# Keys and queries interleaved in DRAM and loaded with one transfer per operand, and the first stage of a hybrid attention layer in another order

## The chip, the cores and the metric

The kernel runs on one core of a Trainium2 chip. The metric is the device time of one launch, in microseconds (us), as the median of several runs; profiles are of one execution. The core has five engines that work side by side, each through its own instructions in order: TensorE (PE, matmuls and transposes; its weight loads are listed as PEld), VectorE (DVE), ScalarE (ACT), GpSimd (POOL), and SyncE (SP), which here does nothing but issue DMA transfers. A DMA issue on SP waits for the eighth issue before it, because eight hardware counters are used in turn.

## What is computed

The reference is one inference step of an encoder layer, on a prompt of 2048 tokens and a sample of 64 tokens that attends to 512 cached ones. It is cut here to what matters:

```python
h = rmsnorm(x, g_pre)
fq, fk, fv, ff, fg, dq, dk, dv, dg = split(h @ w_in)          # widths 512, ff: 8
logf = log_sigmoid(ff + b_f); cum = cumsum(logf)
# group A, 8 heads of 64: forgetting attention, causal
s = fq . fk / 8 + cum[query] - cum[key];      fox = softmax(s) fv
# group B, 4 heads, two halves of 64 for queries and keys, values of 128, causal by chunks of 64
p = softmax(q1 . k1 / 8 + t5_bias) - lam * softmax(q2 . k2 / 8 + t5_bias)
diff = rmsnorm(p dv, subln) * (1 - lam_init)
y = x + rmsnorm(concat(fox * silu(fg), diff * silu(dg)) @ w_out, g_post)
```

The outputs are y for the prompt and the sample, and the new rows of fk, fv, logf, dk and dv. Everything is float32. The width of the model is 1024.

## The kernel before, in words

**Precision.** TensorE works here on values rounded to a shorter form, so each operand is split into a rounded part h and the rest l, and a product is made of three matmuls (lines 868 to 870: wh and x's h, wl and x's h, wh and x's l). In the scores a key operand holds h and l of 64 dimensions in its 128 partitions; it is multiplied with a query tile that holds (h|l) and with one that holds (l|h), line 351.

**Stages.** The prompt is four blocks of 512 tokens, each of four tiles of 128; the sample is a fifth tile of block 0. For each block the projection goes through eight groups of 512 columns: fv, fg, fk, fq, dg, dk, dq, dv in the even blocks, reversed in the odd ones. A group has eight slices of 128 input rows; a slice of weights is loaded (`wst` in block 0, `wraw` later, line 773), cast by ACT to `wh` (line 776), and the rest `wl` is made by DVE or POOL (line 777). The tokens' slices `xraw` become `xx` (lines 744 to 748). In block 0 the first group is accumulated for all tiles at once as slices come in; its forget logits follow (lines 1096 and 1097), with sums of squares `ptq` (line 1071), the 1/rms `xrs` (lines 154 to 157) and its transposed copy `ptr` (line 1055), which is written to DRAM (RS) and loaded again over all partitions as `rbc`. In the other blocks the sums of squares come from loads `xn` (lines 1036 and 1037).

**Results on their way.** Evictions (`ef`, line 878) go out, and their h and l parts to scratch in DRAM: keys turned over by TensorE (`ptk`, line 959), split as `khl` and written to KS; values to VS; queries, which leave TensorE already turned, scaled by `rbc` (`qf`), split as `qhl` (lines 1013 to 1017) and written to QD (line 1019); gates to GS; the running sum of log-forget to CUM. `khl`, `qhl` and `vhl` share a pool of two buffers, `ef`, `xn`, `qf` and others one of four. An eviction that takes a buffer waits until the DMA that read it has landed.

**Attention.** A block's attention runs beside the next block's projection; the output projection runs beside the last block's. What to load is asked for per head and pair of query tiles, and queued in rings: K 4 tiles of 1024 keys, V 4, Q 6 tiles of 256 columns, bias 2, gates 2. A K tile takes a load per 512 keys (line 194), a query pair takes one load for (h|l) (line 267) and two of 64 partitions for (l|h) (line 270), a bias tile a load per 512 keys (line 285). All these go through SP's one queue, with the weights and the writes.

**What sets the order.** Every piece of work is put on a line of places measured in TensorE time, and the pieces are issued in that order; a scheduler then orders each engine's instructions. Constants are loaded in `prologue` (place 20) and `prologue2` (place 110): the latter loads `lamt` and `cbias` (lines 1358 and 1370). The forget bias `fb` and the scale `subl` are loaded at the very start from ACT's queue, `fb` with

```python
nc.scalar.dma_start(out=fb, in_=bass.AP(fbias.tensor, fbias.offset, [[0, P], [0, 5], [1, 8]]))
```

which is 128 x 5 = 640 pieces of 32 bytes, and DVE scales `subl` right away (line 119). The output projection's weights `wor` are cast in place of the projection's operands (lines 1199 to 1201) as the last block's attention runs alone.

Of the kernel before, what the change touches and what calls it, by code (L numbers as in the profile page):

```python
# [9 lines left out]
F32 = mybir.dt.float32  # L10
# [7 lines left out]
P = 128  # L18
# [15 lines left out]
# T5 bucket of rel = key - query over the runs of rel in which it is constant  # L34
# (NUM_BUCKETS = 32, MAX_DISTANCE = 128, bidirectional); every rel below -90 is bucket 15.
# [7 lines left out]
LINE = BW + P - 1  # L43


class Ring:
    """Loads that run ahead of their use, as many as there are free slots."""
# [43 lines left out]
def hybrid_step(ctx: ExitStack, tc: tile.TileContext, ins, outs):  # L91
# [23 lines left out]
    fb = cp.tile([P, 40], F32, name="fb")  # L115
    nc.scalar.dma_start(out=fb, in_=bass.AP(fbias.tensor, fbias.offset, [[0, P], [0, 5], [1, 8]]))
    subl = cp.tile([P, 1], F32, name="subl")
    nc.scalar.dma_start(out=subl, in_=subln)
    nc.vector.tensor_scalar(out=subl, in0=subl, scalar1=1.0 - LAM_INIT, scalar2=None, op0=ALU.mult)
# [15 lines left out]
    QD = [dr.tile([2, 8, P, BLK + (DEC if b == 0 else 0)], F32, name=f"QD{b}") for b in range(NBLK)]  # L135
# [4 lines left out]
    CUM = [dr.tile([8, BLK], F32, name=f"CUM{b}") for b in range(NBLK)]  # L140
# [5 lines left out]
    def rsqrt_newton(pool, v, out, rows, n, tag, eng=None):  # L146
        """out = 1/sqrt(v): exp(-ln(v)/2) and one Newton step."""
# [11 lines left out]
    # ------------------------------------------------------------------ attention  # L159
    class Attn:  # L160
        """Attention of one range of query tiles, over every unit (two fox heads or one diff head)."""
# [38 lines left out]
        def want_kc(self, got, u):  # L200
            """The sample's keys of a unit: both heads' operands, the cached ones and the new ones."""
# [13 lines left out]
            def second():  # L215
# [5 lines left out]
                # the order of the parts doesn't matter  # L221
# [38 lines left out]
        def want_q(self, got, u, hd, col, w):  # L260
            def load(s):
                def go():
                    t = self.p["q"].tile([P, 256], F32R, name="qg", tag="q")
                    src = QD[0] if col >= SEQ else QD[col // BLK]
                    c0 = BLK if col >= SEQ else col % BLK
                    if s == 0:
                        nc.sync.dma_start(out=r32(t[:, :w]), in_=src[hd, u, :, c0:c0 + w])
                    else:
                        for a in (0, 64):
                            nc.sync.dma_start(out=r32(t[a:a + 64, :w]), in_=src[hd, u, 64 - a:P - a, c0:c0 + w])  # L270
                    got.append(t)
                return go
            for s in (0, 1):
                self.want(self.Q, load(s))

        def want_cum(self, got, h, nk, sample):
            def load(c0, w):
                def go():
# [3 lines left out]
                    else:  # L282
                        for a in range(c0, c0 + w, BLK):
                            ww = min(BLK, c0 + w - a)
                            nc.sync.dma_start(out=t[:, a - c0:a - c0 + ww],
                                              in_=bcast_row(CUM[a // BLK][h, 0:ww], ww))
# [5 lines left out]
        def want_strip(self, got, h, nk, sample):  # L292
            """The bias of the last columns up to the diagonal; before them it is that of bucket 15."""
# [46 lines left out]
            # chunks of at most a bank, none narrow where that can be avoided  # L340
# [46 lines left out]
        def store_mix(self, mix, u, pair, w):  # L387
            """mix: f32 [128 mix columns, w tokens], in SBUF."""
            nc.sync.dma_start(out=(MN if pair is None else MS[pair])[u], in_=mix[:, :w])

        # ---- sub-jobs: (A thunks, B thunks, thunks of the step after)
        def fox(self, u, hd, pair, ctxu, first, last, sample=False):
            """One head, one pair of query tiles (or the sample's tile)."""
# [7 lines left out]
            for j, t in enumerate(tiles):  # L401
# [14 lines left out]
                if j == len(tiles) - 1:  # L416
                    def endA():
                        self.Q.free(); self.Q.free()
# [1084 lines left out]
```

## Time and profile before

| | us |
|---|---|
| runs | 1832.17, 1841.0, 1841.08 |
| median | 1841.0 |
| span of the profiled execution | 1837.8 |
| PE busy in it | 1736.8 |
| DVE, ACT, POOL busy | 1189.6, 1128.9, 768.2 |
| data moved by DMA | 361.38 MB |

The profiled execution's own time isn't listed apart from its span. How to read the lines further down: a row of the timeline has start and duration in us, engine, line of the kernel, operation, output <- inputs, shapes, and in brackets the idle time of that engine just before it and what ended it (`<-DMA x<-y` is a transfer's landing, `<-ACT ef L878` an instruction on another engine). A row of windows has a stretch, its length, the busy time (and count) of PE, PEld, DVE, ACT and POOL, the clock granted to TensorE as a share of full speed, the mean busy share of the 16 DMA engines, and GB/s. A row for a line, such as L1201, has the least, median and greatest duration in ns. A row of DMA issues has the count, KB each, and the median time to landing.

### The profile page before, as it was taken

The page shows a single profiled execution, that of the slowest core. Times are in us where ns is not written, and L with a number is a line of the kernel's source. Part 1 is how long each engine was busy: PE and PEld are TensorE (multiplying, and loading weights), DVE is VectorE, ACT ScalarE, POOL GpSimd, SP SyncE. Part 2 cuts the span into 40 slices and gives each one's busy share as a digit, 9 for nine tenths or more (in the row PEclk, how much of TensorE's full clock was granted, in tenths as well). Part 3 has the DMA queues.
Part 4 walks back from the last instruction along what each step waited for, and adds up shares of the span by engine and source line. Part 5 has one row for each costly group of instructions (what it writes and reads, how often), then busy time and mean ns, then how long its engine had stood idle before and what let it go on. Part 6 is the DMA issues. An engine that isn't in the chain of part 4 may idle for free. (4 is left out here: it accounts for less than half of the span.)

```text
span 1837.8 us, 31858 instructions
## 1 busy us (share of the span) xinstructions
PE 1736.8 (95%) x9828; PEld 1467.4 (80%) x9828; DVE 1189.6 (65%) x3274; ACT 1128.9 (61%) x2518; POOL 768.2 (42%) x1083
## 2 busy tenths in 40 slices
PE   7888999999999999989999999999989999999998
PEld 5676888777877778878888888888878878887887
DVE  5422555556668576656776678878867876666764
ACT  4533656465767666665666657667776666556663
POOL 2204235345354453343323225555795663322331
PEclk9998999999999999999999999999989999999999
DMA  7787579789868766867777667667665464455433
GB/s 203 240 193 193 162 217 273 205 245 233 218 209 246 213 196 195 233 170 230 219 229 224 177 181 216 195 195 224 199 219 166 145 189 156 153 181 156 145 115 108
DMA packets 308170, 361.38 MB, mean 197 GB/s; under 512 B 41808, under 2 KB 202732, under 8 KB 308000
## 3 DMA queue, kind: packets, MB, share of 16 engines
q1 hardware_dynamic: 306384, 356.93, 66.9%
q0 software_dynamic: 672, 2.38, 0.4%
q8 instruction: 79, 1.29, 0.3%
q14 instruction: 91, 0.75, 0.1%
q10 hardware_dynamic: 944, 0.03, 0.0%
HBM read 263.89 MB, written 97.70 MB: 197 GB/s over the span
## 5 line engine op out<-in xcount | busy, mean ns | idle before, releaser
L372 ACT ACTIVATE prob<-prob,mn 128x1024 f32<-128x1024 f32 (+8 forms) x400 | 356.1, 892 | 180.7 <-DVE mn L359 179.5
L351 PE MATMUL S<-kg,qg 128*128 128x512 f32 (+4 forms) x1344 | 375.8, 373 | 20.5 <-DVE mn L359 10.0
L497 DVE TENSOR_TENSOR ptl<-pt,pth 128x512 fp32r<-128x512 f32 (+3 forms) x456 | 284.4, 636 | 94.8 <-ACT pth L496 92.3
L868 PE MATMUL acc<-wh,xx 128*128 128x512 f32 x752 | 303.4, 408 | 18.9 <-ACT wh L776 14.9
L869 PE MATMUL acc<-wl,xx 128*128 128x512 f32 x752 | 300.6, 401 | 8.5 <-DVE wl L777 8.5
L870 PE MATMUL acc<-wh,xx 128*128 128x512 f32 x752 | 300.6, 400 | 0.1
L496 ACT CAST pth<-pt 128x512 fp32r<-128x512 f32 (+3 forms) x456 | 237.6, 545 | 81.9 <-PE pt L490 65.4
L351 PEld LDWEIGHTS S<-kg,qg 128*128 128x128 f32 (+1 forms) x1344 | 226.6, 188 | 62.0 <-DVE mn L359 18.8
L490 PE MATMUL pt<-ident,prob 128*128 128x128 f32 (+2 forms) x1692 | 257.6, 274 | 4.7 <-ACT pts L637 2.2
L490 PEld LDWEIGHTS pt<-ident,prob 128*128 128x128 f32 (+2 forms) x1692 | 200.2, 142 | 26.6 <-ACT pts L637 3.3
L777 POOL TENSOR_TENSOR wl<-wraw,wh 128x512 fp32r<-128x512 f32 x126 | 167.4, 1345 | 121.2 <-ACT wh L776 91.0
L408 POOL TENSOR_TENSOR dg<-bias,cmask 128x128 f32<-128x128 f32 (+1 forms) x136 | 66.1, 486 | 281.8 <-DVE mn L359 188.4
L868 PEld LDWEIGHTS acc<-wh,xx 128*128 128x128 f32 x752 | 144.2, 193 | 49.7 <-ACT wh L776 17.2
L869 PEld LDWEIGHTS acc<-wl,xx 128*128 128x128 f32 x752 | 144.6, 192 | 37.3 <-DVE wl L777 11.5
L521 PE MATMUL av<-pth,vg 128*128 128x256 f32 (+1 forms) x576 | 158.3, 294 | 9.4 <-DVE oT L537 4.7
L870 PEld LDWEIGHTS acc<-wh,xx 128*128 128x128 f32 x752 | 144.0, 191 | 28.4 <-DVE xx L745 0.6
L521 PE MATMUL av<-ptl,vg 128*64 128x256 f32 (+1 forms) x576 | 140.3, 283 | 3.9 <-DVE ptl L497 3.6
L776 ACT CAST wh<-wraw 128x512 fp32r<-128x512 f32 x168 | 100.5, 618 | 69.1 <-DMA wraw<-in_w_in 59.9
L359 DVE CUSTOM_DVE_ANT_0 prob<-S,bias,mn 128x512 f32<-128x512 f32 (+4 forms) x200 | 115.3, 577 | 28.8 <-DMA bias<-CUM 14.5
L521 PE MATMUL avd<-pth,vg 128*128 128x256 f32 (+1 forms) x576 | 131.6, 288 | 2.3 <-ACT pth L496 2.3
L521 PEld LDWEIGHTS av<-pth,vg 128*128 128x128 f32 x576 | 110.0, 191 | 21.5 <-issue 7.7
L453 POOL TENSOR_SCALAR gate<-gate,rr 128x64 f32<-128x64 f32 (+1 forms) x136 | 61.5, 463 | 140.2 <-DMA gate<-GS 57.9
(257 smaller groups left out, 3611.8 us busy)
## 6 DMA issues: line engine op xcount, KB each, us to landing
wraw<-in_w_in SPq DMA_DIRECT2D x168, 256.0 KB, 4.8
vg<-VS SPq DMA_DIRECT2D x80, 512.0 KB, 4.1
kg<-KS SPq DMA_DIRECT2D x160, 256.0 KB, 4.1
bias<-CUM SPq DMA_DIRECT2D x80, 256.0 KB, 5.6
wst<-in_w_in SPq DMA_DIRECT2D x64, 256.0 KB, 5.6
out<-ef SPq DMA_DIRECT2D x64, 256.0 KB, 3.3
VS<-vhl SPq DMA_DIRECT2D x32, 512.0 KB, 4.6
KS<-khl SPq DMA_DIRECT2D x64, 256.0 KB, 4.7
```

What stands on the lines that cost most here:

```text
L351: nc.tensor.matmul(S[:rows, :c1 - c0], q()[s][:, qc:qc + rows], kg()[ki][:, c0 - k0:c1 - k0], start=(s == 0), stop=(s == 1))
L359: nc.vector.tensor_tensor_reduce(out=pr[:rows, a - p0:b - p0], in0=S[:rows, a - c0:b - c0], in1=ap()[:rows, a - b0:b - b0], scale=1.0, sca ...
L372: nc.scalar.activation(out=pr, in_=pr, func=AF.Exp, scale=-1.0, bias=st["m"][:rows, i - 1:i], accum_out=st["s"][:rows, h:h + 1])
L490: nc.tensor.transpose(pt[:rk, off:off + rows], self.key_tile(sts[j], rows, kt, rk), ident[:rows, :rows])
L496: nc.scalar.copy(h[:rk, :off], pt[:rk, :off])
L497: nc.vector.tensor_tensor(out=l[:rk, :off], in0=pt[:rk, :off], in1=r32(h[:rk, :off]), op=ALU.subtract)
L521: nc.tensor.matmul(st["av"][:vs.stop - vs.start, j0 * rows:W], ctxu["v"][kt // 4][:rk, kt % 4, vs], g["p"][part][:rk, o:o + w], start=(kt ...
L776: nc.scalar.copy(h, raw[:, :BLK])
L777: (nc.vector if many or k % 4 == 3 else nc.gpsimd).tensor_tensor(out=l, in0=raw[:, :BLK], in1=r32(h), op=ALU.subtract)
L868: nc.tensor.matmul(a, x[0][:, c0:c0 + rows], wh, start=s, stop=False)
L869: nc.tensor.matmul(a, x[0][:, c0:c0 + rows], wl, start=False, stop=False)
L870: nc.tensor.matmul(a, x[1][:, c0:c0 + rows], wh, start=False, stop=e)
```

## The change

It does the following.

1. KS is one DRAM tile in which a row (one of 64 of a head, for 8 units) holds h and l side by side for all tokens. A K tile is one load, and a tile's keys are written with one DMA of 128 partitions instead of two of 64. K loads go from 160 to 96.
2. QD holds h, l and h again for each 256 tokens, so that one load of 128 x 512 brings both query operands: 128 loads instead of 128 + 256 for the prompt, 32 instead of 48 for the sample. The Q ring has 3 tiles of twice the width. An eviction writes h once more (lines 1047 and 1048 of the changed kernel), half as many bytes again; in block 0 a head pair's 576 columns are cut as 256 and 256 + 64 rather than 288 and 288, and the sample's part goes to a tile QN of its own, which makes 24 writes of 16 in each of block 0's two query groups.
3. CUM is one tile, and a bias tile one load: 48 for 80.
4. `fb` is 128 x 8 and loaded in `prologue` through SP; `subl` is loaded and scaled in `prologue2`; `row` of block 0 comes after the third tile of fg; fg's first two tiles use other banks; 16 matmuls on zeros (`idle`) stand at the front of TensorE's queue.
5. Key transposes with their split and write (`k_turn`) are apart from the eviction. In block 0 they come four slices into the next tile's matmuls (or the first query piece's); elsewhere at once.
6. `xn` is loaded one ahead of its use.
7. w_out's slices come in the order 4 to 7, 0 to 3; for the first four ACT scales and casts in one operation, and DVE makes the rest, where ACT scaled, ACT cast and POOL made the rest.

The rest of the diff removes comments. Its core:

```diff
-    KS = [dr.tile([2, 8, P, BLK], F32, name=f"KS{b}") for b in range(NBLK)]
+    KS = dr.tile([P, 8, 2, SEQ], F32, name="KS")
-    QD = [dr.tile([2, 8, P, BLK + (DEC if b == 0 else 0)], F32, name=f"QD{b}") for b in range(NBLK)]
+    QD = [dr.tile([8, P, 3 * BLK], F32, name=f"QD{b}") for b in range(NBLK)]
+    QN = dr.tile([8, P, 3 * DEC], F32, name="QN")
-    CUM = [dr.tile([8, BLK], F32, name=f"CUM{b}") for b in range(NBLK)]
+    CUM = dr.tile([8, SEQ], F32, name="CUM")
...
-                    for c in range(k0, k1, BLK):
-                        nc.sync.dma_start(out=r32(t[:, c - k0:c - k0 + BLK]), in_=KS[c // BLK][hd, u])
+                    nc.sync.dma_start(out=r32(t[:, :k1 - k0]), in_=KS[hd * 64:hd * 64 + 64, u, :, k0:k1])
...
+                    c0 = 3 * (col % BLK)
+                    a = QD[col // BLK][u, rows, c0:c0 + 2 * w]
+                    nc.sync.dma_start(out=r32(t[:, :2 * w]),
+                                      in_=bass.AP(a.tensor, a.offset, [a.ap[0], [w, 2], a.ap[1]]))
+                got.extend((t[:, :w], t[:, w:2 * w]))
...
-                    th += g0[:-1] + first[:1] + f + g0[-1:] + first[1:]
+                    th += g0[:-1] + first[:1] + f + g0[-1:]
+                    row0 = first[1:]
+                        if b == 0 and gi == 1 and tt[0] == tl[2]:
+                            th += row0
...
+            if g in ("fk", "dk"):
+                mine = [(0.4, lambda t=t: self.k_turn(g, t, fs[t], cols[t][1])) for t in ts]
+                if b:
+                    th += [(0.0, fn) for _, fn in mine]
+                else:
+                    self.turn[b] = mine
+            return th[:4] + turn + th[4:]
...
+                            nc.scalar.copy(v[:, :, 0], fs)
+                            nc.vector.tensor_tensor(out=v[:, :, 1], in0=fs, in1=r32(v[:, :, 0]), op=ALU.subtract)
+                            nc.sync.dma_start(out=d[:, :, 2 * m:], in_=r32(v[:, :, 0]))
+                            nc.sync.dma_start(out=d[:, :, :2 * m],
+                                              in_=r32(v).rearrange("p a v t -> p a (v t)"))
...
+    nc.vector.memset(r32(wf), 0.0)
+    idle = ps.tile([P, BLK], F32, name="idle", tag="pt", bufs=3)
+    for _ in range(WARM):
+        nc.tensor.matmul(idle[:, :256], wf.rearrange("p k c -> p (k c)")[:, :P],
+                         wf.rearrange("p k c -> p (k c)")[:, :256], start=True, stop=True)
...
-    caps = (4, 4, 6, 2, 2)
+    caps = (4, 4, 3, 2, 2)
```

Three places show how instructions move. A row is a line of that kernel, an operation, output <- inputs and a shape. The first is DVE at the start of the program; `xx` are the tokens' slices, `wl` the weights' rests. Before:

```order
L745 SCALAR_TENSOR_TENSOR xx<-xraw,gcol,xx 128x576
L748 SCALAR_TENSOR_TENSOR xx<-xraw,gcol,xx 128x64
L119 TENSOR_SCALAR subl<-subl 128x1
L777 TENSOR_TENSOR wl<-wst,wh 128x512
L745 SCALAR_TENSOR_TENSOR xx<-xraw,gcol,xx 128x576
```

And in the changed kernel, there:

```order
L743 SCALAR_TENSOR_TENSOR xx<-xraw,gcol,xx 128x576
L746 SCALAR_TENSOR_TENSOR xx<-xraw,gcol,xx 128x64
L775 TENSOR_TENSOR wl<-wst,wh 128x512
L743 SCALAR_TENSOR_TENSOR xx<-xraw,gcol,xx 128x576
L746 SCALAR_TENSOR_TENSOR xx<-xraw,gcol,xx 128x64
```

The scaling of `subl` no longer stands ahead of the first `wl`. The second place is DVE at the end of block 0's first group; `xv` are the means of squares from `ptq`, `rt` and `xrs` the steps of the 1/rms. Before:

```order
L777 TENSOR_TENSOR wl<-wst,wh 128x512 x2
L1371 TENSOR_SCALAR cbias<-cbias 128x4
L777 TENSOR_TENSOR wl<-wst,wh 128x512 x2
L1076 TENSOR_SCALAR xv<-ptq 128x4
L1076 TENSOR_SCALAR xv<-ptq 64x1
L154 TENSOR_TENSOR rt_453<-xrs 128x8
```

And in the changed kernel:

```order
L775 TENSOR_TENSOR wl<-wst,wh 128x512 x2
L1404 TENSOR_SCALAR subl<-subl 128x1
L1420 TENSOR_SCALAR cbias<-cbias 128x4
L775 TENSOR_TENSOR wl<-wst,wh 128x512 x2
L1114 TENSOR_SCALAR xv<-ptq 128x4
L1114 TENSOR_SCALAR xv<-ptq 64x1
```

`subl` stands here now, and `cbias` stands ahead of `xv` in both. The third place is ACT at the passage from fq to dg in block 0; `qhl` is the rounded part of an evicted query piece, `wh` are dg's weights, `lame` belongs to lambda. Before:

```order
L1015 CAST qhl<-qf 128x288 x6
L776 CAST wh<-wst 128x512
L1015 CAST qhl<-qf 128x288
L776 CAST wh<-wst 128x512
L1364 ACTIVATE lame<-lame 128x2
L776 CAST wh<-wst 128x512 x6
L1015 CAST qhl<-qf 128x288
```

And in the changed kernel:

```order
L1045 CAST qhl<-qf 128x64
L1045 CAST qhl<-qf 128x256
L1413 ACTIVATE lame<-lame 128x2
L1045 CAST qhl<-qf 128x256
L1045 CAST qhl<-qf 128x64
L774 CAST wh<-wst 128x512
L1045 CAST qhl<-qf 128x256
L774 CAST wh<-wst 128x512 x7
```

Six evictions stand ahead of dg's first `wh` in both; `lame` moved ahead of it, and a piece of 256 + 64 columns is two casts.

More of the change, by code (lines that the diff above doesn't have):

```diff
@@ L43 @@
 LINE = BW + P - 1
+WARM = 16
 class Ring:
@@ L114, in hybrid_step @@
     nc.vector.memset(eps_c, EPS)
-    fb = cp.tile([P, 40], F32, name="fb")
-    nc.scalar.dma_start(out=fb, in_=bass.AP(fbias.tensor, fbias.offset, [[0, P], [0, 5], [1, 8]]))
+    fb = cp.tile([P, 8], F32, name="fb")
     subl = cp.tile([P, 1], F32, name="subl")
-    nc.scalar.dma_start(out=subl, in_=subln)
-    nc.vector.tensor_scalar(out=subl, in0=subl, scalar1=1.0 - LAM_INIT, scalar2=None, op0=ALU.mult)
     neglam = cp.tile([P, 1], F32, name="neglam")
@@ L260, in want_q, with go @@
         def want_q(self, got, u, hd, col, w):
[L261 to L274, printed above, removed]
+            def go():
+                t = self.p["q"].tile([P, 512], F32R, name="qg", tag="q")
+                rows = slice(hd * 64, hd * 64 + 64)
+                if col >= SEQ:
+                    for o in (0, 64):
+                        nc.sync.dma_start(out=r32(t[o:o + 64, :2 * w]), in_=QN[u, rows, o:o + 2 * w])
+                else:
[4 more added lines that the diff above has]
+                got.extend((t[:, :w], t[:, w:2 * w]))
+            self.want(self.Q, go)
         def want_cum(self, got, h, nk, sample):
@@ L282, in go @@
                     else:
[L283 to L286, printed above, removed]
+                        nc.sync.dma_start(out=t[:, :w], in_=bcast_row(CUM[h, c0:c0 + w], w))
                     got.append(t)
@@ L604, in endA @@
             def endA():
-                for _ in range(4):
+                for _ in range(2):
                     self.Q.free()
@@ L911, in go @@
                         if k == 0:
-                            a[t] = self.acc(b)
+                            a[t] = self.acc(b, b == 0 and g == GROUPS[1] and t < 2)
                         self.nat_mm(a[t], x[k], w[k], t, cols, k)
@@ L966, in k_out @@
             nc.vector.tensor_tensor(out=l, in0=x, in1=r32(h), op=ALU.subtract)
-            for i, a in enumerate((0, 64)):
-                nc.sync.dma_start(out=sc[i, u0:u0 + 4, :, r0:r0 + rows].rearrange("u (s r) t -> r (u s) t", s=2),
-                                  in_=r32(hl[a:a + 64, :, :rows]))
+            if t == 16:
+                for i, a in enumerate((0, 64)):
+                    nc.sync.dma_start(out=KN[i, u0:u0 + 4].rearrange("u (s r) t -> r (u s) t", s=2),
+                                      in_=r32(hl[a:a + 64, :, :rows]))
+            else:
+                nc.sync.dma_start(out=KS[:, u0:u0 + 4, :, t * P:(t + 1) * P].rearrange("r u s t -> r (u s) t"),
+                                  in_=r32(hl[:, :, :rows]))
         def g_out(self, g, t, f, rows):
@@ L986, in qgroup @@
             u0 = 0 if g == "fq" else 4
-            nb = 1 if nt <= BLK else 2
-            N = nt // nb
+            pieces = [[(0, 2, 256)]] if nt <= BLK else [[(0, 1, 256)], [(256, 1, 256), (BLK, 1, DEC)]]
             th = []
@@ L991, in qgroup, with step @@
                 e = {}
-                for i in range(nb):
-                    def step(k, c=c, i=i, e=e):
+                for i, segs in enumerate(pieces):
+                    t0 = segs[0][0]
+                    N = sum(n * m for _, n, m in segs)
+                    def step(k, c=c, i=i, e=e, t0=t0, N=N):
                         def go():
@@ L1003, in go @@
                             nc.tensor.matmul(o, wl[:, cs], xh[:, xs_], start=False, stop=(k == KC - 1))
-                            if c == 3 and i == nb - 1 and freew:
+                            if c == 3 and i == len(pieces) - 1 and freew:
                                 self.W.free()
                         return go
-                    th += [(3 * N / 2400.0, step(k)) for k in range(KC)]
-                    def evac(c=c, i=i, e=e):
+                    if (c, i) == (0, 0):
+                        turn, self.turn = self.turn.get(b, []), {}
@@ L1010, in evac @@
+                    mm = [(3 * N / 2400.0, step(k)) for k in range(KC)]
+                    th += mm[:4] + (turn if (c, i) == (0, 0) else []) + mm[4:]
+                    def evac(c=c, i=i, e=e, segs=segs, t0=t0, N=N):
                         f = self.p["e"].tile([P, BLK], F32, name="qf", tag="ef")
                         hl = self.p["e"].tile([P, 2 * BLK], F32R, name="qhl", tag="er", bufs=2)
-                        h, l = hl[:, :N], hl[:, N:2 * N]
-                        nc.vector.tensor_tensor(out=f[:, :N], in0=e[i][:, :N], in1=st["rbc"][:, i * N:(i + 1) * N],
+                        nc.vector.tensor_tensor(out=f[:, :N], in0=e[i][:, :N], in1=st["rbc"][:, t0:t0 + N],
@@ L1047, in col @@
                 st["rs"] = rs
-            return [(0.0, square(i, t, hf)) for i, t in enumerate(tl) for hf in (0, 1)] + [(0.0, col)], [(0.1, lambda: self.row(b, st))]
+            return [(0.0, square(n)) for n in range(len(todo))] + [(0.0, col)], [(0.1, lambda: self.row(b, st))]
         def row(self, b, st):
@@ L1181, in weights @@
         def weights(self):
-            self.w = []
+            self.w = {}
             th = []
-            for k in range(KC):
+            for k in (4, 5, 6, 7, 0, 1, 2, 3):
                 def go(k=k):
```

68 lines of the change are left out of this document (44 added, 24 removed).

## The prediction

> **What bounds the kernel now.** I read the page first, then the windows by stage, then PE's waits by line, and last the timeline at each wait that the change touches. The page's first row says which engine the span hangs on:
>
> ```profile
> PE 1736.8 (95%) x9828; PEld 1467.4 (80%) x9828; DVE 1189.6 (65%) x3274; ACT 1128.9 (61%) x2518; POOL 768.2 (42%) x1083
> ```
>
> The windows (PE, PEld, DVE, ACT, POOL busy, granted clock, DMA share, GB/s) say where PE isn't at work, and where its clock is low:
>
> ```profile
> 0.00:60.00 60.00, 44.97 (x182) 33.88 (x183) 27.33 (x53) 27.21 (x49) 14.99 (x19) 0.94 0.83 238
> 60.00:160.00 100.00, 83.60 (x433) 70.85 (x432) 34.77 (x73) 43.15 (x89) 23.87 (x40) 0.91 0.75 188
> 340.00:700.00 360.00, 336.98 (x1811) 275.54 (x1811) 234.98 (x642) 233.89 (x588) 162.74 (x267) 0.98 0.78 219
> 700.00:1300.00 600.00, 582.86 (x3447) 498.01 (x3446) 429.01 (x1246) 392.74 (x854) 241.71 (x323) 0.99 0.72 207
> 1300.00:1400.00 100.00, 94.05 (x506) 79.32 (x505) 73.70 (x185) 74.06 (x157) 78.03 (x73) 0.93 0.68 214
> 1400.00:1838.00 438.00, 414.95 (x2482) 358.08 (x2479) 300.01 (x815) 255.07 (x557) 174.70 (x250) 0.99 0.48 149
> ```
>
> PE is idle 1837.8 - 1736.8 = 101.0 us: 15.0 in the first 60 us, 16.4 in the next 100, 23.0 + 17.1 + 6.0 + 23.1 in the other rows. Busy time times (1 - clock) is what the low clock costs: 2.7 + 7.5 + 6.7 + 5.8 + 6.6 + 4.1 = 33 us. The change adds and removes almost no real matmul, so about 134 us is all that there is to win. PE's waits by line (us in total, times, longest) name the candidates:
>
> ```profile
> PE acc L868 <- ACT wh L776: 14.9, 7, 5.9
> ...
> PE acc L869 <- DVE wl L777: 8.5, 2, 5.0
> PE ptk L959 <- ACT ef L878: 5.8, 4, 3.0
> PE S L351 <- DMA qg<-QD: 5.8, 6, 2.5
> ...
> PE ptr L1055 <- DVE xrs L157: 3.7, 1, 3.7
> ...
> PE av L521 <- DMA vg<-VS: 2.5, 1, 2.5
> ```
>
> These rows sum to 41 us. Most of this stands in the first 160 us and at q loads, where the change works. The sum is made against the span, 1837.8 us; the median of the runs, 1841.0, lies 3.2 above.
>
> **The start.** DVE reaches the first wl late:
>
> ```profile
> 12.56 0.15 DVE L119 TENSOR_SCALAR subl<-subl 128x1 f32<-128x1 f32 x1 [6.77 <-DMA subl<-in_subln]
> ...
> 47.67 0.17 DVE L1371 TENSOR_SCALAR cbias<-cbias 128x4 f32<-128x4 f32 x1 [5.49 <-DMA cbias<-in_relT]
> 47.78 1.29 DVE L777 TENSOR_TENSOR wl<-wst,wh 128x512 fp32r<-128x512 f32 x2
> 48.99 0.21 DVE L1076 TENSOR_SCALAR xv<-ptq 128x4 f32<-128x4 f32 x2
> ```
>
> ```profile
> 13.38 0.80 PE L869 MATMUL acc<-wl,xx 128*128 128x512 f32 x1 [5.01 <-DVE wl L777]
> ...
> 50.64 0.37 PE L1055 MATMUL ptr<-ident,xrs 128*8 128x128 f32 x1 [3.71 <-DVE xrs L157]
> 51.27 0.79 PE L868 MATMUL acc<-wh,xx 128*128 128x512 f32 x1 [0.26 <-ACT ef L878]
> ```
>
> ```profile
> 4.00:9.00 5.00, 2.50 (x5) 1.49 (x5) 1.01 (x2) 1.82 (x3) 0.00 (x0) 1.00 0.05 5
> 9.00:12.00 3.00, 0.00 (x0) 0.00 (x0) 0.00 (x0) 0.77 (x1) 0.00 (x0) 1.00 0.78 266
> ```
>
> From 4 to 9 us the DMA engines move 5 GB/s, while the 640 tiny pieces of fb drain ahead of everything; subl lands behind them, and DVE, in order, can't start wl. With fb a fifth as long and later, and subl's scaling moved behind group 0, the wait of 5.01 goes. Later fb's 128 pieces cost DMA about 5.0 x 128/640 = 1.0 us. The idle matmuls stand before PE's first work and may leave it warm; that is worth something only if group 0's end matters, and it doesn't wholly: the next gate is cbias. The row step itself (ptr, the RS write, the rbc load and POOL's scaling) goes behind a tile of fg; its only readers are fq's evictions, some 80 us on, so it costs nothing there. It landed at 47.67, paced by the DMAs and wl casts before it; 5.0 earlier and 1.0 back makes 43.7, and two wl and xv (1.7 us) follow: 45.4. Before, fg began at 51.27, behind xv, the rsqrt chain and ptr. Now it needs only the bank that xv frees. So 51.27 - 45.4 = 5.9: **-6**. If the cover (group 0's matmuls) is longer than that, -5; if cbias comes earlier too, -8.9 (both gaps and 0.26).
>
> **fk's transposes.** ptk follows its own tile's eviction and PE waits. In the change it stands four steps into the next tile:
>
> ```profile
> 100.00:110.00 10.00, 6.61 (x22) 5.19 (x23) 1.38 (x2) 3.49 (x7) 1.26 (x1) 0.74 0.37 117
> ```
>
> ```profile
> 105.83 0.63 ACT L1037 ACTIVATE xn<-xn 128x512 f32<-128x512 f32 x1 [4.00 <-DMA xn<-in_xp]
> ```
>
> ACT's ef stands behind an xn load of 4.00 us, which the prefetch also moves ahead. The window's 22 PE instructions took 6.61 us, 0.30 each, so four steps of three matmuls cover 12 x 0.30 = 3.6 us, more than the longest wait, 3.0; without that cover the whole wait is back. The KS write moves with the transposes, one issue instead of two; who may wait for it is told under fq. Gap 10.0 - 6.61 = 3.4 in this window, 5.8 in the whole row; the clock costs 6.61 x 0.26 = 1.7. Between -3.4 and -7.5; I take **-6.5**, as nothing else there is late.
>
> **fq to dg.** This is the sharpest doubt.
>
> ```profile
> 151.39 1.22 PE L868 MATMUL acc<-wh,xx 128*128 128x512 f32 x2 [4.43 <-ACT wh L776]
> 156.54 0.79 PE L869 MATMUL acc<-wl,xx 128*128 128x512 f32 x1 [3.50 <-DVE wl L777]
> ```
>
> ```profile
> 138.28 0.43 ACT L1015 CAST qhl<-qf 128x288 fp32r<-128x288 f32 x1 [9.08 <-DMA KS<-khl]
> ```
>
> ```profile
> 155.38 0.23 DVE L1361 CUSTOM_DVE_ANT_0 lamt<-lamt 128x64 f32<-128x64 f32 x1 [3.51 <-DMA lamt<-in_lams]
> ```
>
> ```profile
> 150.00:160.00 10.00, 5.11 (x12) 3.60 (x13) 5.81 (x17) 5.64 (x12) 10.00 (x26) 0.53 0.61 132
> ```
>
> ```profile
> L1019 SPq DMA_DIRECT2D QD<-qhl x80: 574/610/1852, 139.2 to 1217.1; - x80
> ```
>
> dg's first wh casts stand on ACT behind six qhl evictions, each of which waits for its two-deep buffer's DMAs to land. Those become 2 and 4 per eviction, 24 for 16: 8 x 0.61 = +4.9 us of issues, and tile 3's khl is written a little later. Against it: one KS write less before the first cast, single K and q loads between the Q writes on SP, and lamt's load moved ahead, so 3.50 may go. Bounds: all of the loss goes, 4.9 idle + 5.11 x 0.47 = 7.3 us; or the issues come on top with a clock that stays cold, +6. Twelve casts for eight on ACT are inside that bound. I take **0**, near the middle.
>
> **q and K loads.**
>
> ```profile
> kg<-KS SPq DMA_DIRECT2D x160, 256.0 KB, 4.1
> ...
> qg<-QD SPq DMA_DIRECT2D x128, 128.0 KB, 3.1
> qg<-QD SPq DMA_DIRECT2D x256, 64.0 KB, 4.0
> ```
>
> ```profile
> 358.00:364.00 6.00, 4.63 (x20) 3.61 (x21) 1.72 (x6) 3.00 (x8) 0.00 (x0) 0.73 0.58 183
> ```
>
> Three DMAs per query pair become one of 256 KB (nearest row: K's, 4.1 us, against 4.0 for the last of three), so the operand is complete two issues earlier; 160 K loads become 96, 80 bias loads 48. The ring holds as many bytes in 3 slots as in 6, and both operands of a pair are let go together before as now. Q writes grow by half, about 8.4 MB of the page's 361, and PE doesn't wait for writes here. The six q waits are 5.8 us; in this window alone the clock costs 4.63 x 0.27 = 1.3 more, of the stage's 6.7. From 0 (the loads start no earlier, since they wait for PE to free a slot) to 5.8 + 6.7 = -12.5; I take **-7**: most of the waits and two such windows. The one wait for values, 2.5, is behind the same queue: **-1**. A rule of the Trainium skill ("TensorE: Matmul & The Clock Gate", Part 1) has the clock fall only after an idle window of about 3.4 us; by it the gaps here, 2.5 at most, would cost no clock, and this term would be some 2.6 us smaller. The window with 0.73 disagrees, and the measurement decides.
>
> **w_out's operands, and the rest.**
>
> ```profile
> 1355.00:1380.00 25.00, 19.81 (x88) 16.09 (x89) 16.99 (x44) 19.70 (x40) 22.62 (x20) 0.73 0.69 218
> ```
>
> ```profile
> L1201 POOL TENSOR_TENSOR wox<-wor,wox x8: 1282/1298/1302, 1344.5 to 1377.8; 128x512 fp32r<-128x512 f32 x8
> ```
>
> POOL is full here and PE loses 5.2 idle + 19.81 x 0.27 = 5.3. Eight POOL operations of 1.30 go (10.4 us of 22.6) and eight ACT scalings; DVE gets eight. From 0 to -10.5, taken **-4**: the attention's own chains share the window. The xn prefetch in other blocks: **-1**; it holds one ef buffer longer, which is part of the next term. Against all this the scheduler reshuffles an order that fits the present waits; idle time outside the named waits is 101 - 41 = 60 us, and 5 to 10% of it coming anew is **+4**.
>
> Sum: -6 - 6.5 + 0 - 7 - 1 - 4 - 1 + 4 = -21.5. Span 1816.3; time 1841.0 - 21.5 = **1819.5**.
>
> **The rivals.** *The waits only move* (0.20): the K, q and w_out terms come to nothing, because loads start when PE frees a slot, and fk's shrinks to 3.4: -6 - 3.4 + 4 = -5.4, 1835.6. For it: DMA share of 0.7 to 0.8 in the stages, so the next transfer in the queue is late next. Against it: the q waits come in a stage where three issues per pair stand in one queue.
>
> *Spread-out K rows are slow* (0.07), the other side. The K scratch puts a row's next tokens beside it, but the 64 rows of a load now lie 128 KB apart (8 units x 2 parts x 2048 x 4 bytes), where before they were one solid piece. If that halves the rate, each of 96 loads lands some 4.1 us later, 394 us of latency in all, mostly behind a ring of four tiles. It decides from the point where 31 us of this, 8%, reaches PE: 22 to cancel the gain and 9 to be seen. At 10%, +39: 1858. Against it: of 128 q pairs' 4 us (512 us) just 5.8, 1%, reached PE. The Trainium skill ("DMA: Bandwidth & Descriptors", Latency and other measured facts) says that rows a large power of two apart slow copies: 207 GB/s at a pitch of 512 KiB, 103 at 4 MiB, 214 when padded. By it a pitch of 128 KiB would cost nearly nothing; no run here shows such a pitch yet.
>
> *Every cover holds* (0.15): -8.9 - 7.5 - 7.3 - 12.5 - 2.5 - 4 = -43, and some new stalls, say +8: 1806.
>
> *The forecast* has the rest, 0.58.
>
> **How the numbers follow.** Half a per cent, 9 us, is about what a measurement of this kernel can tell from no change: faster is below 1831.8, slower above 1850.2. The forecast's own range, by fq to dg (-7 to +6) and half of the q and w_out bounds, is 1807 to 1830. Faster: 0.58 of the forecast less a tail of 0.04, 0.15, and a quarter of the first rival: 0.74. Same: the tail and the rest of that rival, 0.19. Slower: 0.07. The range, with the third rival inside and most of the first: 1803 to 1838.
>
> **What would show it.** Right: no PE gap before the first matmul with wl; fg begins between 44 and 47 us; no wait of ptk in fk; S's wait for qg under 2 us; the clock in the w_out window above 0.8. Wrong: dg's wh and wl waits together above 10 us; q waits unchanged, which makes the first rival right; PE waiting for kg, or kg landing above 6 us, which makes the second.

## The result, and the profile after

The changed kernel takes 1786.8 us (median of four runs, 1783.8 to 1787.7), the kernel before 1839.4 on the same chip. The ratio is 0.973, with a 95% interval of 0.970 to 0.976: 52.6 us less, where 21.5 were forecast, from the median of 1841.0 that the first three runs gave, and the range ended at 1803. The span of the profiled execution is 1785.6 us.

The first row of the page after, busy time by engine:

```profile
PE 1721.1 (96%) x9844; PEld 1466.6 (82%) x9844; DVE 1207.3 (68%) x3290; ACT 1127.5 (63%) x2518; POOL 767.9 (43%) x1075
```

PE is idle 1785.6 - 1721.1 = 64.5 us, 36.5 less than before, and it is busy 15.7 us less, though the 16 idle matmuls add 3.8. Part of that is the clock: the mean granted clock of the two executions is 0.982 and 0.987, which is some 9 us of the busy time (an estimate); the rest isn't explained. To see where the time was won, I went through PE's matmuls and transposes in order of their start, without the idle ones, and added up the columns of their shapes. The table says when the one starts that reaches a share of the whole:

| share of PE's work | before, us | after, us | difference |
|---|---|---|---|
| 0.025 (fg begun) | 62.2 | 51.4 | -10.8 |
| 0.05 (late in fk) | 112.3 | 104.4 | -7.9 |
| 0.10 (in dk) | 204.2 | 196.8 | -7.4 |
| 0.175 (block 1 begun) | 327.6 | 319.8 | -7.8 |
| 0.25 | 468.3 | 446.9 | -21.4 |
| 0.35 | 652.7 | 625.6 | -27.1 |
| 0.45 (in block 2) | 850.7 | 814.3 | -36.4 |
| 0.725 | 1325.6 | 1288.3 | -37.3 |
| 0.75 (w_out's operands made) | 1380.9 | 1338.2 | -42.7 |
| 1.0 | 1830.9 | 1778.6 | -52.3 |

The first stage kept some 7.8 of the 10.8 us that it had won. The stretch from there to share 0.45, in blocks 1 and 2, where q and K loads feed the attention beside the projection, won 28.6; from 0.45 to 0.725 it was 0.9, then 5.4 at the output weights and 9.6 in the last stage. The windows of after say the same (columns as before):

```profile
0.00:60.00 60.00, 55.09 (x249) 43.00 (x250) 29.07 (x57) 31.41 (x59) 17.76 (x23) 0.97 0.89 257
60.00:160.00 100.00, 87.46 (x444) 74.88 (x443) 38.31 (x77) 45.27 (x93) 30.60 (x51) 0.91 0.79 214
340.00:700.00 360.00, 349.33 (x1928) 290.39 (x1926) 245.33 (x680) 248.54 (x613) 170.66 (x276) 0.99 0.77 235
```

From 340 to 700 PE was idle 23.0 us and is now idle 10.7, at a clock of 0.99 instead of 0.98, and with nearly the same DMA share (0.77 for 0.78) the DMA engines move 235 GB/s instead of 219. PE's waits by line in the changed kernel:

```profile
PE acc L869 <- ACT wh L774: 8.4, 4, 4.6
...
PE ptk L974 <- ACT ef L879: 6.5, 2, 4.9
...
PE ptf L1186 <- DVE fz L1178: 3.6, 1, 3.6
...
PE acc L869 <- DVE xv L1114: 1.3, 1, 1.3
...
PE S L348 <- DMA qg<-QD: 1.3, 2, 0.7
```

The wait for the first wl is gone, S's wait for queries fell from 5.8 to 1.3, the wait for wh from 14.9 to 8.4. ptk's wait is not gone: 6.5 for 5.8. The timeline of PE at the start of the changed kernel:

```profile
5.46 0.74 PE L869 MATMUL acc<-wh,xx 128*128 128x512 f32 x2 [0.36 <-ACT wh L774]
6.04 0.63 PE L869 MATMUL accS<-wh,xx 128*128 128x512 f32 x2
6.50 0.40 PE L866 MATMUL accS<-wh,xx 128*128 128x512 f32 x1
6.74 0.39 PE L870 MATMUL acc<-wl,xx 128*128 128x512 f32 x1
...
42.55 0.47 PE L869 MATMUL acc<-wh,xx 128*128 128x512 f32 x1 [1.31 <-DVE xv L1114]
```

From 6.5 on one matmul takes 0.39 to 0.40 us, which is the full clock, and the two at 6.04 take 0.63 together, where before such a pair took 1.05 at 6.89. There is no gap before the first wl. fg begins at 42.55, where it was 51.27 before and 45.4 in the forecast.

Of the landing times on the page after, three matter:

```profile
vg<-VS SPq DMA_DIRECT2D x80, 512.0 KB, 6.0
qg<-QD SPq DMA_DIRECT2D x128, 256.0 KB, 4.2
kg<-KS SPq DMA_DIRECT2D x64, 512.0 KB, 5.9
```

K's rows, now 128 KB apart, land as fast as values of the same size in a layout that wasn't changed. Values landed in 4.1 us before; why they take longer now wasn't looked into. The K loads of half the size, 256 KB like all of those before, are in the view of DMA issues. They land sooner than the 4.1 us of before:

```profile
kg<-KS SPq DMA_DIRECT2D x32, 256.0 KB, 3.4
```

### The profile page after: what moved, and what is told of

It reads as the page before. It is cut to its first block, busy times and chain, and to the rows that moved or that the text cites. A ratio compares the mean times of both kernels' runs of the same rounds, so it can differ in the third digit from the quotient of the medians.

```text
span 1785.6 us, 31342 instructions
## 1 busy us (share of the span) xinstructions
PE 1721.1 (96%) x9844; PEld 1466.6 (82%) x9844; DVE 1207.3 (68%) x3290; ACT 1127.5 (63%) x2518; POOL 767.9 (43%) x1075
## 3 DMA queue, kind: packets, MB, share of 16 engines
q1 hardware_dynamic: 278000, 365.57, 66.7%
## 5 line engine op out<-in xcount | busy, mean ns | idle before, releaser
L348 PE MATMUL S<-kg,qg 128*128 128x512 f32 (+4 forms) x1344 | 371.3, 372 | 10.5 <-DVE mn L356 7.2
L450 POOL TENSOR_SCALAR gate<-gate,rr 128x64 f32<-128x64 f32 (+1 forms) x136 | 63.6, 478 | 180.0 <-DMA gate<-GS 85.3
L774 ACT CAST wh<-wraw 128x512 fp32r<-128x512 f32 x168 | 100.4, 621 | 55.5 <-DMA wraw<-in_w_in 44.7
```

What stands on the lines that cost most here:

```text
L348: nc.tensor.matmul(S[:rows, :c1 - c0], q()[s][:, qc:qc + rows], kg()[ki][:, c0 - k0:c1 - k0], start=(s == 0), stop=(s == 1))
L774: nc.scalar.copy(h, raw[:, :BLK])
```

## The experiments

The question was where the 40 us come from that the first stage doesn't explain. Theory A: the loads themselves, fewer pieces in SP's queue. Theory B: only that a query pair is whole sooner. Theory C: the scheduler, which times each DMA, arrives at a better order with fewer of them. Theory D, added later: bias loads. Ratios are to the kernel before, measured beside it on the same chip; 0.1% is 1.8 us. The changed kernel itself gave 0.9732, again on another chip 0.9746 (0.971 to 0.978), and with its order held 0.9720 (0.970 to 0.974); 0.973 is the yardstick.

**Parts put back, the scheduler free.** Three kernels; the new layout, the tiles and the bytes stay.

```diff
-                    nc.sync.dma_start(out=r32(t[:, :2 * w]),
-                                      in_=bass.AP(a.tensor, a.offset, [a.ap[0], [w, 2], a.ap[1]]))
+                    rs = a.ap[0][0]
+                    nc.sync.dma_start(out=r32(t[:, :w]),
+                                      in_=bass.AP(a.tensor, a.offset, [a.ap[0], [w, 2], [1, w]]))
+                    for o in (0, 32):
+                        nc.sync.dma_start(out=r32(t[2 * o:2 * o + 64, w:2 * w]),
+                                          in_=bass.AP(a.tensor, a.offset + o * rs + w, [[rs, 32], [w, 2], [1, w]]))
```

> The changed kernel, with each query pair of the prompt loaded in three DMAs again (one of 128 partitions for the first operand, two of 64 for the second), from the new layout and into the same tile: 256 more issues on SP, the same bytes. Theory A (the gain in blocks 1 and 2 comes from fewer issues in SP's one queue, which brings every load in it sooner): about +15 us on 1786.8, with more waits of all kinds, at least 1800. Theory B (it comes from the query pair being whole sooner, nothing else): +20, and waits of S for qg back to about 6 us. Theory C (the new order happens to fit better, the loads hardly matter): within 8 us of 1787, in either direction.

```diff
-                    nc.sync.dma_start(out=r32(t[:, :k1 - k0]), in_=KS[hd * 64:hd * 64 + 64, u, :, k0:k1])
+                    for c in range(k0, k1, BLK):
+                        nc.sync.dma_start(out=r32(t[:, c - k0:c - k0 + BLK]),
+                                          in_=KS[hd * 64:hd * 64 + 64, u, :, c:c + BLK])
```

and likewise for the bias loads (512 keys each) and the KS writes (64 partitions each):

> The changed kernel, with a K tile and a bias tile loaded per 512 keys again and a tile's keys written in two DMAs of 64 partitions: 64 + 32 + 32 = 128 more issues on SP, the same bytes and the same layout. Theory A: about +8 us, half of what the query loads cost. Theory B: 0 to +3, since no query pair is later. Theory C: within 8 us, either way.

Both diffs together:

> Both: all of SP's issues of before in blocks 1 to 3, with the new layout and the new first stage. Theory A: the sum, +23 us or more, 1810 or above, which leaves the start's and the output weights' part of the gain. Theory B: as with the queries alone, +20. Theory C: not the sum of the two.

Measured: queries in three 0.9852 (0.983 to 0.987), +1.2%, 22 us; K, bias and key writes in two 0.9899 (0.988 to 0.992), +1.7%, 30 us; all 0.9967 (0.995 to 0.998), +2.4%, 43 us. The 30 us of K, bias and key writes are outside of all that was expected of them (about 8 by theory A, 0 to 3 by B, at most 8 by C). One more execution of the kernel with all in parts, a single one, gave 1824.3 beside 1831.4:

> Placeholder for the pair below: the changed kernel in the scheduler's order with q, K, bias and KS writes in parts, once more: 0.997 of the kernel before under every theory.

So the loads in parts give back most of the gain, against B, which had next to nothing for K and bias. But the sum of the two is more than both together, and the order had moved too: TensorE's order differs from the changed kernel's in 2784 rows.

**The old start.**

```diff
-    fb = cp.tile([P, 8], F32, name="fb")
+    fb = cp.tile([P, 40], F32, name="fb")
+    nc.scalar.dma_start(out=fb, in_=bass.AP(fbias.tensor, fbias.offset, [[0, P], [0, 5], [1, 8]]))
...
-    for _ in range(WARM):
...
-                    th += g0[:-1] + first[:1] + f + g0[-1:]
+                    th += g0[:-1] + first[:1] + f + g0[-1:] + first[1:]
...
-                if b:
-                    th += [(0.0, fn) for _, fn in mine]
-                else:
-                    self.turn[b] = mine
+                th += [(0.0, fn) for _, fn in mine]
```

> The changed kernel with the first stage of before: fb's 640 pieces and subl from ACT's queue at the start, no idle matmuls, the row right after the first group, key transposes at once. All theories have the start worth what equal work in the two traces shows, 8 to 14 us: 1795 to 1801. If it is more, part of the gain in blocks 1 and 2 hangs on how the stage before leaves the queues; if less, the start's gain was given back later anyway.

Measured 0.9797 (0.978 to 0.982): +0.6%, 12 us, inside what was expected; by the two intervals it is 3 to 21 us, and equal work in the traces had shown 7.8. Its own trace shows the waits of before at the start:

```profile
13.43 0.80 PE L870 MATMUL acc<-wl,xx 128*128 128x512 f32 x1 [5.08 <-DVE wl L778]
```

**One kind at a time, and empty issues.** The changed kernel again as a yardstick, K in two, bias in two, and 128 DMAs of 4 bytes at the places of the parts:

> The changed kernel itself, as a yardstick beside the next three: 0.973 of the kernel before under every theory.

> The changed kernel with each K tile of 1024 keys loaded in two DMAs of 512 keys, nothing else: 64 more issues. The 128 issues for K, bias and KS writes together cost 1.7% (31 us). If each issue on SP costs the same (theory A), half of that, +15 us, ratio 0.981. If the bias loads are what is waited for (theory D: bias<-CUM ends DVE's and POOL's waits, nobody waits for kg), +0 to +5, ratio below 0.976.

> The changed kernel with each bias tile loaded in two DMAs of 512 keys, nothing else: 32 more issues. Theory A: a quarter of 31 us, +8, ratio 0.977. Theory D: most of it, +20 or more, ratio above 0.984.

```diff
+                    if k1 - k0 > BLK:
+                        nc.sync.dma_start(out=r32(t[:1, 2 * BLK:2 * BLK + 1]), in_=KS[hd * 64:hd * 64 + 1, u, 0, k0:k0 + 1])
...
+                        if w > BLK:
+                            nc.sync.dma_start(out=t[:1, BW:BW + 1], in_=relT[:1, :1])
...
+                nc.sync.dma_start(out=DUM[t:t + 1, u0:u0 + 1], in_=r32(hl[:1, 0, :1]))
```

> The changed kernel with 128 DMAs of 4 bytes more on SP, one behind each K tile load of more than 512 keys, each bias load of more than 512 keys and each KS write; every tile still comes in one load and nothing reads the 4 bytes. Theory A (an issue's place in SP's queue is the price): +25 us or more, like the real split, ratio 0.987 or above. If the price is that a tile's second part lands later, or that packets are shorter: 0 to +6, ratio below 0.977. Theory C (any edit brings another order, and the changed kernel's is a lucky one): +10 to +30 as well, but then the single splits each cost as much as the three together.

Measured: 0.9746 (0.971 to 0.978) for the yardstick; K 0.9815 (0.979 to 0.984), bias 0.9788 (0.976 to 0.982), empty issues 0.9782 (0.975 to 0.981). K alone costs some 13 us, about what theory A had; bias alone and the empty issues overlap with the yardstick. D is out, since bias wasn't the most of it. The empty issues cost less than the real parts, and far less than the 0.987 that theory A asked for. But all of these moved the order as well, so I didn't take more from them.

**Plain order.** The scheduler's simulated times switched off, so that an engine's instructions stand nearly as the line of places has them:

```diff
-    with tile.TileContext(nc, schedule_with_timeline_sim=True) as tc:
+    with tile.TileContext(nc, schedule_with_timeline_sim=False) as tc:
```

> The kernel before, with the scheduler's simulated times switched off, so that each engine's instructions stand nearly as the line of places has them. By itself it says what that scheduling is worth to the kernel before: no theory gives a number; anything from the same to 5% slower.

> The changed kernel, likewise. Theory A (the loads themselves are what is gained: fewer pieces, sooner there): 2% or more faster than the kernel before in plain order. Theory C (the gain is that the scheduler, which times each DMA, arrives at a better order with fewer of them): the difference between the two plain orders is the start's part alone, 0.3 to 0.8%.

> The changed kernel in plain order, with the loads of q, K and bias and the writes of KS in parts as in the run that had all in parts. The order of TensorE differs in 296 rows of 7547 from the plain order of the changed kernel, where with the scheduler it differed in 2784. Theory A: as much slower than the changed kernel in plain order as with the scheduler, some 2.3%. Theory C: less than 0.6%.

Measured: before 1.0614, more than the 5% that was allowed for, after 1.0550, in parts 1.0598 (each within 0.005). The changed kernel gains only 0.6% here, and parts cost 0.5%: by what was written down ahead, this spoke for C. I take it as misleading. In plain order PE is idle 1947.7 - 1782.7 = 165 us before and 1932.1 - 1773.2 = 159 after, 64 and 95 us more than in the scheduler's order. That other waits end last there, and that what the loads are worth is hidden behind them, is argued from these sums; no run shows it.

**The order held.** The scheduler can be told which instruction stands behind which on an engine, without a wait. So I gave it the changed kernel's order as a chain for each engine, with the further parts right behind the first, and in the opposite kernel the order of the one with all in parts. On PE, DVE, ACT and POOL nothing moves, and the traces show it: PE's 9844 rows and those of the other three come in the same order. On SP only the parts come or go.

```diff
+                    tc.add_manual_dep(i, prev.name, info, reason="order")
...
         hybrid_step(tc, ins, outs)
+        pin(tc, nc)
```

> The changed kernel with q, K, bias loads and KS writes in parts (384 more issues on SP), and with the order of every engine's instructions held exactly as in the changed kernel; the further parts stand right behind the first. Theory A (the loads themselves): 0.997 of the kernel before, as when the scheduler was free. Theory C (the order): 0.975 to 0.982, the parts costing the half per cent that they cost in plain order.

> The opposite: loads and writes whole as in the changed kernel, but every engine's order held exactly as the scheduler had it for the kernel with all in parts. Theory A: 0.974, as the changed kernel. Theory C: 0.990 to 0.995, most of the loss without a single further issue.

> The changed kernel, its order held as it is: the yardstick for these three, 0.974.

| | loads whole | loads in parts |
|---|---|---|
| order of the changed kernel | 0.9720 (0.970 to 0.974) | 0.9983 (0.996 to 1.000) |
| order found for the parts | 0.9799 (0.977 to 0.983) | 0.9967 (0.995 to 0.998) |

This tells the loads from the order. In one and the same order the parts cost 2.6% (1832.5 - 1784.7 = 48 us), and in the other order 1.7% (31 us; the fourth ratio was measured on another chip). The order is worth 0.8% (15.5 us) when the loads are whole; when they aren't, the two ratios overlap, and neither order is shown to be the better one. Theory A holds for most of the 40 us, C for the smaller part at most.

The parts aren't quite the loads of before, though, and the 48 us are likely more than the change saved by its loads. The kernel with all in parts has the new start (12 us) and the new making of w_out's operands (5.4), and yet it is only 6 us faster than the kernel before (0.9967), so elsewhere it is slower by some 11 by these figures. And the stages don't match one by one: by equal work, the parts in the changed kernel's order cost 25.5 us up to share 0.45 and 14 more from there to 0.725, where the change had won 0.9. That stays open. The windows of the two runs with one order, first whole, then in parts:

```profile
340.00:700.00 360.00, 347.33 (x1922) 288.61 (x1921) 245.10 (x675) 247.93 (x613) 170.41 (x277) 1.00 0.77 234
700.00:1300.00 600.00, 592.12 (x3521) 510.00 (x3520) 451.01 (x1274) 404.03 (x878) 263.00 (x333) 1.00 0.71 219
```

```profile
340.00:700.00 360.00, 338.57 (x1811) 277.83 (x1810) 229.52 (x638) 237.60 (x594) 160.34 (x266) 0.98 0.77 223
700.00:1300.00 600.00, 584.12 (x3434) 497.65 (x3433) 435.91 (x1240) 388.86 (x845) 247.74 (x324) 0.99 0.72 212
```

The DMA share is the same, 0.77 and 0.71 to 0.72; PE does 1922 and 1811 instructions from 340 to 700. With the parts PE waits little for the parts themselves (2.4 us for queries in all); other loads that come through SP are waited for longer, though not all (POOL's wait for gates is 82.0 us, and 85.9 with the loads whole). Of the two traces' waits, first whole, then in parts:

```profile
POOL dg L438 <- DMA bias<-CUM: 51.9, 15, 11.1
...
ACT wh L807 <- DMA wraw<-in_w_in: 43.6, 37, 3.1
```

```profile
POOL dg L450 <- DMA bias<-CUM: 76.2, 17, 10.7
...
ACT wh L819 <- DMA wraw<-in_w_in: 60.5, 44, 4.1
```

The weights' own loads, which no part touched, are waited for 17 us more.

**The issue or the data.** In the held order, 384 empty DMAs at the places of the parts, and K, bias and key writes in two with the queries whole:

```diff
+                    for o in (0, 1):
+                        extra(nc.sync.dma_start(out=r32(t[:1, 512 + o:513 + o]),
+                                                in_=QD[col // BLK][u, hd * 64:hd * 64 + 1, c0 + o:c0 + o + 1]))
```

> The changed kernel in its own order, its loads and writes whole, with 384 DMAs of 4 bytes more on SP at just the places where the run with parts in this order had its further parts (two behind each of 128 query loads, one behind each wide K load, wide bias load and KS write). Nothing reads them. If the price of parts is the issue itself, its time in SP's one queue and its turn among the eight counters: 0.990 to 0.998, most of the 48 us. If it is that the parts are real data (a part's landing to be waited for, more and shorter packets): 0.972 to 0.980.

> The changed kernel in its own order with the K and bias loads and KS writes in two (128 more issues), the query loads whole. If every issue costs the same, a third of the 48 us that 384 cost: 16 us, ratio 0.981. If query loads are what matters: below 0.976. If K and bias are: above 0.988.

Measured: 0.9837 (0.981 to 0.987), +1.2% on 0.972, 21 us, for the empty ones; 0.9886 (0.986 to 0.991), +1.7%, 30 us, for K, bias and key writes. These two were measured on another chip than the 0.972, and by the two intervals the 21 us may be 12 to 32. So further issues with hardly a byte account for a bit under half of the 48. The rest goes with the data, and neither outcome that I had written down for the empty ones was met: they fall between. For K, bias and key writes the third one was: above 0.988, they are what matters more. If the costs add up, their 128 parts cost more than the 256 of the queries (48 - 30 = 18). What SP spends on a DMA differs by its form. The query loads of before, of the run with parts, and of the one with empty issues (minimum, median and maximum in ns):

```profile
L267 SPq DMA_DIRECT2D qg<-QD x144: 319/386/1775, 143.2 to 1735.8; - x144
...
L270 SPq DMA_DIRECT2D qg<-QD x288: 444/522/1989, 144.9 to 1737.4; - x144
```

```profile
L312 SPq DMA_DIRECT2D qg<-QD x256: 508/597/1962, 147.7 to 1730.9; - x128
L309 SPq DMA_DIRECT2D qg<-QD x128: 513/565/1707, 147.1 to 1729.7; - x128
```

```profile
L311 SPq DMA_DIRECT2D qg<-QD x256: 214/266/1106, 146.3 to 1705.3; - x128
```

And a tile's key write in the held order, as two of 64 partitions and as one of 128:

```profile
L1029 SPq DMA_DIRECT2D KS<-khl x64: 574/626/1764, 106.5 to 1276.5; - x64
```

```profile
L1020 SPq DMA_DIRECT2D KS<-khl x32: 367/380/932, 104.6 to 1253.4; - x32
```

A query pair took SP 386 + 2 x 522 = 1430 ns before, a key write 2 x 627 (626 here). With all in parts a pair takes 565 + 2 x 597 = 1759 ns, another reason why that run isn't the kernel before. The durations of SP's DMA rows, added up over the whole trace, are 872 us before (47% of the span) and 659 after (37%); in the held order 654 whole, 770 with the empty issues, 753 with K, bias and key writes in two, 918 with all in parts. The time is more by 0, 21, 30 and 48 us. It isn't one price for a microsecond of SP: 21/116, 30/99 and 48/264 lie between 0.18 and 0.30.

Nor is a further issue's price only its time on SP. An issue waits for the landing of the eighth before it, so a further one also takes a place among eight in flight. SP's waits that a landing ended, added up over the trace, are 83 us whole, 142 with the empty issues and 99 with all in parts. How much of the 21 us is SP's time and how much the place in flight, and what the rest of the 48 is, a landing that comes later in two parts or the more and shorter packets (312816 in the run with all in parts, 278000 whole), wasn't separated.

**One named wait.** In the held order, ACT's eviction ahead of the Square in front of it, in block 0's fk group:

> The changed kernel in its own order, but for one move on ACT in block 0's fk group: the eviction for which the key transposes waited 4.9 us stands ahead of the Square that waited 8.6 us for its xn load, and no longer behind it. If that Square is what held the transposes: 5 to 8 us less than the changed kernel (the wait and two to three us of clock), ratio 0.970. If the eviction waits for something else, or block 0 gives it back at the passage to dg: no difference.

Measured 0.9741 (0.971 to 0.977), no difference clear of the intervals. The eviction waits by itself:

```profile
98.76 0.69 ACT L912 ACTIVATE ef<-acc,xrs 128x512 f32<-128x512 f32 x1 [11.01 <-DMA GN<-ef]
```

Its buffer of the pool of four is held until a gate write lands, and SP issues that write only behind an xn load that waits for a buffer itself. In the changed kernel's SP queue the gap stands ahead of that load, from 86.5 to 94.1:

```profile
85.69 0.83 SPq L1001 DMA_DIRECT2D GS<-ef  x1
94.09 0.33 SPq L1064 DMA_DIRECT2D xn<-in_xp  x1
...
95.50 0.46 SPq L1001 DMA_DIRECT2D GN<-ef  x1
```

That load waits for its buffer until a GS write has landed. It did so before the change as well, as long, and with the GN write behind it in the queue; SP's waits before and after:

```profile
SPq L1036 <- DMA GS<-ef: 7.5, 1, 7.5
```

```profile
SPq L1064 <- DMA GS<-ef: 7.5, 1, 7.5
```

So the load at the head of the one queue holds what is behind it in both kernels, and the prefetch changed nothing about it. Whether more buffers would wasn't tried. No version that beats the changed kernel came out of these runs.

## Why the prediction was wrong

The direction was right and the size wasn't: 52.6 us for 21.5.

- **q and K loads: the step that failed.** "The six q waits are 5.8 us; in this window alone the clock costs 1.3 more ... I take -7", and -1 each for values and xn. From block 1's beginning to share 0.45 the traces differ by 28.6 us, where these terms had 9 in all, and the parts cost 31 to 48 us with the order held. I priced 272 query, 64 K and 32 bias issues, and 32 key writes, by the waits of PE that ended on a load of queries or values. But SP's queue feeds everything. Of PE's 23.0 us of idle time from 340 to 700, 6.4 named q loads, and 1.4 do now; of the others, which named the exponentials' chain (mn, ptl, pts), gates, weights or evictions, 16.6 became 9.3. That these had waited for something that came through the same queue is shown for some of it: from before to after ACT's waits for weights fell from 59.9 to 44.7 us and DVE's for bias from 24.3 to 18.3, but POOL's for gates rose from 57.9 to 85.3. The bound I should have put at the upper end is all idle time of the stages that the queue feeds: 23.0 + 17.1 in the rows from 340 to 1300, and 6.7 + 5.8 of clock.
- **New stalls, +4.** They didn't come; idle time outside the named waits fell too. The scheduler refits its order to the loads; the changed kernel's order is worth 15.5 us over the one found for the parts, with the loads whole.
- **The rival "the waits only move"** rested on the DMA share of 0.7 to 0.8. The share is a mean over 16 engines and hardly changed (0.78 and 0.77); what counted was the number of issues, by SP's time or the eight places in flight, and that has no row on the page.
- **The start, -6.** Measured -8.7 at fg's first matmul, 51.27 to 42.55. The gate that I named held: DVE still stands idle for the constants ahead of xv. But they landed by 40.69, where I had worked out 43.7, and PE lost 1.31 us to it:

```profile
40.69 0.15 DVE L1404 TENSOR_SCALAR subl<-subl 128x1 f32<-128x1 f32 x1 [6.32 <-DMA subl<-in_subln]
40.87 0.17 DVE L1420 TENSOR_SCALAR cbias<-cbias 128x4 f32<-128x4 f32 x1
```

  In all the first stage is worth 12 us by the run with the old start.

- **fk's transposes, -6.5.** Wrong: the wait is 6.5 us for 5.8, of it 4.9 in fk as one wait, where there were two of 5.0 together, and the stage gave back 2.9 us (shares 0.025 to 0.05). I named ACT's wait for an xn load, and that the prefetch moves it ahead. But the first xn load stands in SP's queue where it stood, held for 7.5 us, with a write behind it that frees a buffer of the eviction's pool. Four slices later the eviction that the transposes need still isn't there.
- **fq to dg, 0.** Right in sum, 7.9 won at share 0.05 and 7.4 at 0.10, but by luck: dg's waits for wh and wl fell from 7.9 to 2.5 us, and a new one came at the next group, dk, where before it was 0.3. ACT's casts stand there behind an xn load:

```profile
170.27 0.63 ACT L1075 ACTIVATE xn<-xn 128x512 f32<-128x512 f32 x1 [8.83 <-DMA xn<-in_xp]
...
173.36 0.79 PE L869 MATMUL acc<-wh,xx 128*128 128x512 f32 x1 [4.60 <-ACT wh L774]
```

- **w_out's operands, -4.** Measured -5.4 between shares 0.725 and 0.75, inside its bounds. The operands are made from 1302.5 to 1335.4 in the changed kernel. The window of their first half has the full clock; in the next one PE is idle 3.7 us, of it 3.24 for DVE's prob (line 596), and the clock is 0.93:

```profile
1296.00:1321.00 25.00, 23.88 (x147) 20.88 (x145) 22.94 (x53) 21.63 (x47) 17.74 (x19) 1.00 0.77 242
1321.00:1346.00 25.00, 21.35 (x112) 17.74 (x113) 20.02 (x47) 16.64 (x37) 20.87 (x20) 0.93 0.60 189
```

- **The last stage, nothing.** It won 9.6 us. K and bias loads of block 3 and the output projection's loads stand in the same queue, and with the order held the parts cost 11.5 us from share 0.75 on; I had no term for it.
- **Spread-out K rows.** Didn't happen: 512 KB of K land in 5.9 us, of V in 6.0, and 256 KB of K in 3.4, where it was 4.1. The Trainium skill ("DMA: Bandwidth & Descriptors", Latency and other measured facts) has no pitch below 512 KiB, at which it gives 207 GB/s, and nothing here speaks against that.

## What to carry to other kernels

Where one engine issues nearly all transfers, add up its issue time before anything else. Here it was 872 of 1838 us, and whole loads were worth 31 to 48 us with the order held, where the waits that named queries and values added up to 8.3. To tell such a cause from the order that a scheduler finds, hold the order fixed and change only the loads; in a plain order with more waits of its own the effect hardly showed. A load in an in-order queue that waits for a free buffer holds up what is behind it, 7.5 us here, and asking for it earlier didn't help.

## What the runs showed of the hardware

A DMA of 4 bytes that nothing reads takes SP 0.27 us behind a query load (median), and 384 of them cost this kernel 21 us, with 59 us more of SP waiting for landings. One DMA of 128 partitions takes SP less time than one of 64 with half as many bytes: 0.38 us against 0.63 for the key writes. And sixteen matmuls on zeros, from 1.32 to 5.10 us, brought the full clock by the first real ones: two at 6.04 took 0.63 us together and the next one 0.40, where before such a pair took 1.05 at 6.89, the matmul at 13.38, behind a gap of 5.01, took 0.80, and the first at 0.39 came at 19.48.
